# Attention queries on one core: the rotary rows of eight heads gathered into one tile, the split into two parts made from PSUM, and the heads put together again over DRAM

## The chip, the core and the metric

The kernel runs on one core of one Trainium2 chip. The metric is the device time of one launch in microseconds (us). Engines are named as in the profile: PE multiplies matrices, DVE is the vector engine, ACT the scalar engine with its function tables, POOL the GpSimd engine, SP issues DMA transfers. SBUF is the on-chip memory, PSUM the memory into which PE accumulates.

## What is computed

The reference is a decoder trunk of two layers on 1024 tokens of width 1024, in float32. Per layer:

```python
h = rmsnorm(x, norm_mix[l])
q, k, v, u, ug, ga, gb = jnp.split(h @ w_in[l], SPLITS, axis=-1)
q = partial_rope(rmsnorm(q, q_norm[l]), cos, sin)   # 16 heads of 64; the first 16 dims of each rotate
k = partial_rope(rmsnorm(k, k_norm[l]), cos, sin)   # 2 key heads, each for 8 query heads
a_out = sliding_window_attention(q, k, v, sinks[l]) # window 128, blocks of 128 queries
c_out = conformer_conv(u, ug, ...)                  # GLU, causal depthwise conv of width 31, LayerNorm, swish
x = x + (sigmoid(ga) * a_out + sigmoid(gb) * c_out) @ w_out[l]
g, up = jnp.split(rmsnorm(x, norm_ffn[l]) @ w_gate_up[l], 2, axis=-1)
x = x + (silu(g) * up) @ w_down[l]
```

`partial_rope` turns dims 0 to 7 of a head against dims 8 to 15, by an angle that depends on the token, and leaves dims 16 to 63 as they are.

## The kernel before

Everything is kept transposed: features on the 128 partitions, the 1024 tokens along the free axis. To keep float32 accuracy at PE's faster float32r rate, an operand is split into a high and a low part, and a product is made of three matmuls (high x high, high x low, low x high).

A layer has three stages: the input projection with attention and convolution beside it (to about 565 us of the span in layer 0), the merge with the output projection, and the feed-forward part. The change lies in the first.

**The first stage.** The projection makes 34 tiles of 128 output features. Each takes eight steps over the width; a step is six matmuls of 128x512. The list `INPROJ` gives the order of the tiles; K and V come first, two tiles (`TAIL`) are left for after the attention. The program is written along a clock of such steps: `tick()` counts one, `after(n, fn)` and `at(when, fn)` let a piece of the other work be written n steps later. PE's and (in this stage) DVE's instructions are executed in the order in which they are written; those of ACT, POOL and SP are arranged by a scheduler. So what stands where on PE and DVE is fixed by a handful of numbers: `SP` steps between attention units, `S0` steps to the first one, `TS` steps between convolution taps, `QSP`, `QN`, `T1`, `T2`, `TD`, `AD` for the parts of a query tile and of a unit.

**A query tile** (`queries`, L581) holds two whole heads. ACT multiplies by the norm's gain into `q32` and squares the tile into `sqh`. `rope` (L380) copies four strips of 8 rows, swapped, to `rot` by DMA, and POOL multiplies `q32` by the cosine table (L385) and `rot` by the sine table (L386), both 128x1024. Seven steps later DVE adds them (L400). ACT copies each head's 64 rows to the high half of `qs[h]` (L609), and DVE subtracts to get the low half (L613), in the same tile's other 64 partitions, two instructions of 64x1024. Beside that PE sums the squares per head (L391), DVE adds the epsilon (L394), and POOL raises to the power -1/2 (L396), which gives the factor `fq`; from it come its negative `nfq` (L596) and the scaled sinks `sr` (L597, L599).

**An attention unit** (`unit_s`, L622) is two heads by two blocks; 32 units a layer, eight pairs of heads by four. PE writes scores into the one PSUM bank `S` (L633, L634). POOL puts the sinks into a column of `sc` (L636), ACT copies the scores of the own block (L638), DVE those of the block before under a mask (`copy_predicated`, L645), then their greatest (L649) and its negative product (L651); ACT takes the exponential (L653), DVE the reciprocal (L658), ACT scales (L660). PE transposes (`pT`, L669), ACT and DVE split (`ph`, L671; `pl`, L676), POOL masks in four instructions (L681, L684), PE multiplies by the values (`po`, L699), ACT and DVE add the two halves (L704, L705, L711). The next unit's scores go into the same bank `S`, so they wait for L645. The sums of squares use the same bank as `po`.

**The convolution** (`conv_taps`, L485) takes one DVE instruction per tap, 31 for each of four channel tiles (L492, L496): `y = a[:, j:j+T] * w[j] + y`, in SBUF. A channel can begin when its gate tile is projected. LayerNorm over the channels follows: `pmu` (L533) the mean, `pssl` the variance, `pb` (L317) spreads a factor over the partitions.

**Gates** are evicted by DVE times the norm's factor (L721). `fetch` (L120) loads weights (`raw`), ACT casts the high part `wh` (L133), POOL subtracts the low part `wl` (L134). All DMA transfers are issued by SP, in one order.

Of the kernel before, what the change touches and what calls it, by code (L numbers as in the profile page):

```python
# [12 lines left out]
F32 = mybir.dt.float32  # L13
# [8 lines left out]
P = 128  # L22
# [18 lines left out]
V_GK = 17  # L41
V_CB = 18
V_LG = 22
V_LB = 26
V_CWT = 30
V_SK = V_CWT + CC * CW
NV = V_SK + NH
# [5 lines left out]
def trunk(ctx, tc, xT, win, wcv, wout, wgu, wdn, vecs, cosT, sinT, outT):  # L53
# [165 lines left out]
    def when_free(bank, n, fn):  # L219
        def go():  # L220
            if bank in busy:
                after(0.25, go)
            else:
                fn()
        after(n, go)
# [95 lines left out]
    for l in range(DEPTH):  # L321
# [32 lines left out]
        ct = mp.tile([P, T], F32, name="ct")  # L354
        st_ = mp.tile([P, T], F32, name="st_")
        nc.sync.dma_start(ct, cosT)
        nc.sync.dma_start(st_, sinT)
# [6 lines left out]
        sB = [dp.tile([P, T], F32, name=f"sB{l}_{i}") for i in range(8)]  # L364
        att = ExitStack()
        ap_ = pool("ap", 1, None, att)
        rot = ap_.tile([P, T], F32, name="rot")
        nc.gpsimd.memset(rot, 0.0)
# [11 lines left out]
        def rope(src):  # L380
            for h in range(2):
                o = h * HD
                nc.sync.dma_start(rot[o:o + 8], src[o + 8:o + 16])
                nc.sync.dma_start(rot[o + 8:o + 16], src[o:o + 8])
            nc.gpsimd.tensor_tensor(out=src, in0=src, in1=ct, op=ALU.mult)  # L385
            nc.gpsimd.tensor_tensor(out=rot, in0=rot, in1=st_, op=ALU.mult)  # L386

        def headnorm(sq, f):
            pss = ps_o("pssh")
            for b in range(NB):  # L390
                nc.tensor.matmul(pss[:, 2 * b:2 * b + 2], sq[:, b * P:(b + 1) * P], blk1,  # L391
                                 start=True, stop=True)
            ssb = sm.tile([P, NB, 2], F32, tag="ssb", name="ssb")
            nc.vector.tensor_tensor(out=ssb, in0=pss[:, 0:16].rearrange("p (b h) -> p b h", h=2),  # L394
                                    in1=e64.unsqueeze(2).broadcast_to([P, NB, 2]), op=ALU.add)
            nc.gpsimd.tensor_tensor(out=f, in0=ssb.rearrange("p b h -> p (b h)"), in1=mhalf, op=ALU.pow)  # L396
            return ssb

        def rope_add(src):
# [7 lines left out]
        def keys(ps):  # L407
# [4 lines left out]
            after(1 if l else NA + 0.5, lambda: rope(k32))  # L412
            f8 = sm.tile([P, 16], F32, tag="f8", name="f8")

            def norm():
                fk = sm.tile([P, 16], F32, tag="fk", name="fk")
                headnorm(sq, fk)
# [26 lines left out]
            after(9, lambda: rope_add(k32))  # L444
# [40 lines left out]
        def conv_taps():  # L485
            for c in range(CC):
# [4 lines left out]
                y = ap_.tile([P, T], F32, tag="y", bufs=1, name="y")  # L491
# [648 lines left out]
AB = 2  # L1140
# [79 lines left out]
```

## Time and profile before

| | |
|---|---|
| runs | 2714.76 us median of 3 (2712.35 to 2716.32) |
| the profiled execution's own time | 2710.93 us |
| its span, first to last instruction | 2709.2 us |
| PE busy | 2585.2 us, 95% |
| DVE busy | 1876.9 us, 69% |
| POOL busy | 1654.0 us, 61% |
| ACT busy | 1196.4 us, 44% |
| mean granted clock of PE | 0.979 |
| DMA | 379.06 MB, 140 GB/s on the mean |

How to read it: the shares are means over stages that differ. PE is busy for nearly the whole of the span outside the two first stages, and there DVE is idle for a third of the time or more. In the first stages, from about 110 to 490 us and from about 1450 to 1830 us, DVE is busy for over nine tenths. Busy time of PE is not work done: a matmul at a lower clock, or one that is overlapped with its neighbour, counts as busy too. So the number of matmuls per microsecond is the better measure.

### The profile page before, as it was taken

Reading aid. Unit: us, or ns where it says so; the run is one execution under the profiler, and the core shown is the slowest. Engines: PE = TensorE matmul, PEld = TensorE weight load, DVE = VectorE, ACT = ScalarE, POOL = GpSimd, SP = SyncE. Lnnn points to the kernel's source line nnn. Section 1 sums busy time; section 2 is a strip of 40 time slices with the busy share of each in tenths; the row PEclk is TensorE's granted clock in tenths of the full one; section 3 lists DMA queues with packets and bytes.
Section 4 is the critical chain, followed back from the end, with each engine's and each line's share of the span. In section 5 each row is a group of like instructions: output and inputs, shape, how many; then the busy total and the mean of one; then the engine's idle time right before and its main releaser. Section 6 shows DMA issues by size and latency. Waiting matters only on the chain. (4 is left out here: it accounts for less than half of the span.)

```text
span 2709.2 us, 33260 instructions
## 1 busy us (share of the span) xinstructions
PE 2585.2 (95%) x11736; PEld 2112.5 (78%) x11736; DVE 1876.9 (69%) x2053; ACT 1196.4 (44%) x2251; POOL 1654.0 (61%) x1092
## 2 busy tenths in 40 slices
PE   7898898999999999999999989899999999999999
PEld 5777777888787888878877767778887788888887
DVE  6689999652468777855637999995616668778344
ACT  2266566843432323344523665668325222223443
POOL 7368787535356777764535778785252677767544
PEclk8999999999999999999999999999999999999999
DMA  3111111375244454476711111114752444455666
GB/s 129 42 51 34 57 64 51 140 264 215 86 165 149 170 179 156 160 276 218 239 57 43 41 57 49 59 63 156 251 202 97 175 167 145 163 179 191 223 224 210
DMA packets 132359, 379.06 MB, mean 140 GB/s; under 512 B 15136, under 2 KB 15392, under 8 KB 132192
## 3 DMA queue, kind: packets, MB, share of 16 engines
q1 hardware_dynamic: 132048, 376.85, 40.6%
q8 instruction: 92, 1.51, 0.2%
q14 instruction: 75, 0.61, 0.1%
q10 hardware_dynamic: 144, 0.09, 0.0%
HBM read 259.17 MB, written 115.34 MB: 138 GB/s over the span
## 5 line engine op out<-in xcount | busy, mean ns | idle before, releaser
L151 POOL TENSOR_TENSOR plo<-fraw,phi 128x512 fp32r<-128x512 f32 x290 | 423.0, 1467 | 229.2 <-ACT phi L149 214.7
L151 POOL TENSOR_TENSOR plo<-fs,phi 128x512 fp32r<-128x512 f32 x160 | 264.3, 1663 | 253.5 <-ACT phi L149 241.7
L496 DVE SCALAR_TENSOR_TENSOR y<-a,vec,y 128x1024 f32<-128x1024 f32 x240 | 405.7, 1690 | 4.0
L134 POOL TENSOR_TENSOR wl<-raw,wh 128x1024 fp32r<-128x1024 f32 (+1 forms) x100 | 252.4, 2525 | 241.7 <-PE ps L242 196.6
L149 ACT CAST phi<-fraw 128x512 fp32r<-128x512 f32 x444 | 257.6, 618 | 246.4 <-POOL plo L151 131.8
L242 PE MATMUL ps<-hx,wh 128*128 128x512 f32 x1056 | 349.1, 412 | 7.3 <-ACT hx L283 7.3
L242 PE MATMUL ps<-hx,wl 128*128 128x512 f32 x1056 | 335.8, 399 | 4.4 <-POOL wl L134 4.4
L242 PE MATMUL ps<-lx,wh 128*128 128x512 f32 x1056 | 338.0, 401 | 0.8 <-DVE lx L284 0.8
L149 ACT CAST phi<-fs 128x512 fp32r<-128x512 f32 x160 | 95.4, 620 | 534.3 <-DVE fs L164 529.1
L151 DVE TENSOR_TENSOR plo<-fraw,phi 128x512 fp32r<-128x512 f32 x154 | 133.6, 873 | 187.8 <-ACT phi L149 185.5
L847 PE MATMUL b<-plo,phi 128*128 128x512 f32 x616 | 240.8, 391 | 3.9 <-DVE plo L151 3.6
L242 PEld LDWEIGHTS ps<-hx,wl 128*128 128x128 f32 x1056 | 204.8, 194 | 50.0 <-POOL wl L134 4.8
L242 PEld LDWEIGHTS ps<-lx,wh 128*128 128x128 f32 x1056 | 206.1, 195 | 47.9 <-DVE lx L284 1.6
L847 PE MATMUL b<-phi,plo 128*128 128x512 f32 x616 | 239.8, 389 | 0.0
L847 PE MATMUL b<-phi 128*128 128x512 f32 x616 | 239.7, 389 | 0.0
L242 PEld LDWEIGHTS ps<-hx,wh 128*128 128x128 f32 x1056 | 195.6, 197 | 42.9 <-ACT hx L283 7.3
L653 ACT ACTIVATE sc<-sc,nm,fq 128x129 f32<-128x129 f32 x256 | 123.7, 486 | 118.0 <-DVE nm L651 117.6
L133 ACT CAST wh<-raw 128x1024 fp32r<-128x1024 f32 (+1 forms) x100 | 98.2, 982 | 166.0 <-PE ps L242 128.3
L915 POOL TENSOR_TENSOR g<-g,u 128x512 f32<-128x512 f32 (+1 forms) x84 | 129.4, 1558 | 31.9 <-DVE u L968 25.5
L911 DVE TENSOR_TENSOR g<-g 128x512 f32<-128x512 f32 x88 | 102.0, 1159 | 65.7 <-POOL g L915 42.5
L847 PEld LDWEIGHTS b<-plo,phi 128*128 128x128 f32 x616 | 115.6, 188 | 31.6 <-DVE plo L151 7.6
L847 PEld LDWEIGHTS b<-phi 128*128 128x128 f32 x616 | 115.6, 188 | 24.2
(254 smaller groups left out, 6219.2 us busy)
## 6 DMA issues: line engine op xcount, KB each, us to landing
fraw<-wgu SPq DMA_DIRECT2D x88, 512.0 KB
raw<-win SPq DMA_DIRECT2D x68, 512.0 KB
act<-g SPq DMA_DIRECT2D x44, 512.0 KB
dw<-wdn SPq DMA_DIRECT2D x44, 512.0 KB
td<-g SPq DMA_DIRECT2D x44, 512.0 KB
sd<-dw SPq DMA_DIRECT2D x44, 512.0 KB
fraw<-sd SPq DMA_DIRECT2D x88, 256.0 KB
fraw<-td SPq DMA_DIRECT2D x88, 256.0 KB
```

The source lines that it names most:

```text
L133: nc.scalar.copy(wh, raw)
L134: nc.gpsimd.tensor_tensor(out=wl, in0=raw, in1=wh.bitcast(F32), op=ALU.subtract)
L149: nc.scalar.copy(hi, src)
L151: (eng or nc.gpsimd).tensor_tensor(out=lo, in0=src, in1=hi.bitcast(F32), op=ALU.subtract)
L242: nc.tensor.matmul(ps[:, sl], a[:, wc], b[:, sl], start=first and j == 0, stop=last and j == 2)
L496: nc.vector.scalar_tensor_tensor(out=y, in0=a[:, j:j + T], scalar=V(w0 + j), in1=y, op0=ALU.mult, op1=ALU.add)
L653: nc.scalar.activation(sc[:, n], sc[:, n], AF.Exp, bias=nm[:, n:n + 1], scale=fq[:, 4 * j + n:4 * j + n + 1], accum_out=den[:, n:n + 1])
L847: nc.tensor.matmul(ps, w[:, ai * P:(ai + 1) * P], x, start=first and j == 0, stop=last and j == 2, skip_group_check=True)
L911: nc.vector.tensor_tensor(out=o, in0=x, in1=y, op=ALU.subtract)
L915: nc.gpsimd.tensor_tensor(out=g[:, sl], in0=g[:, sl], in1=u[:, sl], op=ALU.mult)
```

## The change

The 1024 query columns of the input projection are put in another order on the host. For each group of eight heads the first of four tiles (m = 0) holds the 16 rotated rows of all eight heads, first dims 0 to 7 of each head, then dims 8 to 15; the other three tiles (m = 1 to 3) hold the eight heads' 48 other rows. So two of eight tiles are rotated instead of eight, with two DMA copies of 64 rows each for the swap.

A tile with m > 0 is split straight from PSUM: ACT writes the high part with the gain (`qh`), DVE the low part in one `scalar_tensor_tensor` from PSUM (`ql`, L623 of the new kernel). A tile with m = 0 goes through SBUF: rotary addition on DVE, high part on ACT, low part on DVE (L640). Both parts are stored to DRAM (L615), and `factors` loads each head's 64 high and 64 low rows into `qs[h]` (L677, L678; eight loads per pair of heads), at the earliest when the pair before it has begun. The layout of `qs` is now the same for both heads of a pair.

The sums of squares come from a product with an indicator of the head (eight columns, `V_IN`) and are added up over the tiles in `ssq`. The cosine and sine tables are now loaded into the buffers of `A`; `rot` is one of the four `t4` buffers. The sinks' column is copied by ACT instead of POOL. The bank `po` is marked as busy from the sum of squares to its addition, and `unit_t` also waits for `ph`. A second buffer `y` is given to the convolution (`YB`). `INPROJ` and the distances are new: first unit 14 steps behind its tiles instead of 16 behind the first, `TD` 9 for 7.5, `T2` 4.5 for 3.5, `TS` 1.3 for 1.42.

The diff, cut to its core:

```diff
@@ rope, headnorm
-        def rope(src):
-            for h in range(2):
-                o = h * HD
-                nc.sync.dma_start(rot[o:o + 8], src[o + 8:o + 16])
-                nc.sync.dma_start(rot[o + 8:o + 16], src[o:o + 8])
-            nc.gpsimd.tensor_tensor(out=src, in0=src, in1=ct, op=ALU.mult)
-            nc.gpsimd.tensor_tensor(out=rot, in0=rot, in1=st_, op=ALU.mult)
+        def rope(src, swaps, ts):
+            rot = t4("rot")
+            if len(swaps) > 2:
+                nc.gpsimd.memset(rot, 0.0)
+            for o, i, n in swaps:
+                nc.sync.dma_start(rot[o:o + n], src[i:i + n])
+            nc.gpsimd.tensor_tensor(out=src, in0=src, in1=ts[0], op=ALU.mult)
+            nc.gpsimd.tensor_tensor(out=rot, in0=rot, in1=ts[1], op=ALU.mult)
+            return rot
...
@@ queries
-            def split():
-                rope_add(q32)
-                for h in range(2):
...
-                    nc.scalar.copy(qs[h][hi], q32[hi])
...
-                    after(1.5 + h, lambda hi=hi, lo=lo, h=h: nc.vector.tensor_tensor(
-                        out=qs[h][lo], in0=q32[hi], in1=qs[h][hi].bitcast(F32), op=ALU.subtract))
...
+        def queries(t, ps):
+            g, m = t // 4, t % 4
+            gain = V(V_GQ + m)
...
+            def store(*x):
+                for w in range(2):
+                    dst = qn[g][w, (m - 1) * P:m * P] if m else qr[g][w].rearrange("s h r t -> (s h r) t")
+                    nc.sync.dma_start(dst, x[w])
+                arrived(g, m)
+            if m:
...
+                nc.scalar.activation(hi, ps, AF.Copy, scale=gain)
+                nc.scalar.activation(sq, ps, AF.Square)
+
+                def rest():
+                    nc.vector.scalar_tensor_tensor(out=lo, in0=ps, scalar=gain, in1=hi.bitcast(F32),
+                                                   op0=ALU.mult, op1=ALU.subtract)
+                    store(hi.bitcast(F32), lo.bitcast(F32))
+                after(QL, rest)
+            else:
...
+                rot = rope(q32, [(0, HD, HD), (HD, 0, HD)], qtab)
+
+                def split():
+                    rope_add(q32, rot)
+                    hi = t4("q0h")
+                    nc.scalar.copy(hi.bitcast(F32R), q32)
+                    after(1.5, lambda: low(hi))
+
+                def low(hi):
+                    nc.vector.tensor_tensor(out=q32.bitcast(F32R), in0=q32, in1=hi, op=ALU.subtract)
+                    store(hi, q32)
+                after(QSP, split)
...
+        def factors(g, p):
+
+            i = 4 * g + p
+            if units_done[0] < 4 * (i - 1):
+                after(1, lambda: factors(g, p))
+                return
...
+            for h in range(2):
+                hh = 2 * p + h
+                for w in range(2):
+                    q = qs[h].bitcast(F32)
+                    nc.sync.dma_start(q[w * HD:w * HD + 16], qr[g][w, :, hh])
+                    nc.sync.dma_start(q[w * HD + 16:(w + 1) * HD], qn[g][w, hh * 48:(hh + 1) * 48])
...
@@ unit_s
-            nc.gpsimd.tensor_copy(sc[:, :, P], sr[:, 2 * j:2 * j + 2].rearrange("p b h -> p (b h)"))
+            nc.scalar.copy(sc[:, :, P], sr[:, 2 * j:2 * j + 2].rearrange("p b h -> p (b h)"))
...
@@ constants
-INPROJ = [W_K, W_V, _u[0], _ug[0], 0, _u[1], _ug[1], 1, _gb[0], _u[2], 2, _ug[2], _ga[0], 3, _gb[1], _ga[1],
-          4, _u[3], _ga[2], 5, _ug[3], _ga[3], 6, _gb[2], _ga[4], 7, _gb[3], _ga[5], _gb[4], _gb[5],
-          _ga[6], _ga[7], _gb[6], _gb[7]]
+INPROJ = [W_K, W_V, _u[0], _ug[0], 1, 0, 4, 2, _u[1], 3, _ug[1], _ga[0], _u[2], 5, _ug[2], _ga[1], 6, _gb[0], _ga[2],
+          7, _ga[3], _u[3], _ug[3], _ga[4], _gb[1], _gb[2], _ga[5], _gb[3], _gb[4], _ga[6], _gb[5], _ga[7],
+          _gb[6], _gb[7]]
...
-TD, AD = 7.5, 5.5
-S0 = 16
+TD, AD = 9, 5.5
+S0 = 14
+YB = 2
+QL, QN2 = 1.5, 1.5
...
-T1, T2, SCB = 2.2, 3.5, 2
+T1, T2, SCB = 2.2, 4.5, 2
...
-TS = 1.42
+TS = 1.3
```

Line numbers in the prediction are those of the kernel before, but for L487, L505, L615, L623, L640, L677, L678 and those in the rows of the new order, which are lines of the changed kernel.

More of the change, by code (lines that the diff above doesn't have):

```diff
@@ L220, in go @@
         def go():
-            if bank in busy:
+            if busy & set(bank.split()):
                 after(0.25, go)
@@ L411, in keys @@
             nc.scalar.activation(sq, ps, AF.Square)
-            after(1 if l else NA + 0.5, lambda: rope(k32))
+            ts = tables(cosT, sinT)
+            swaps = [(h * HD + a, h * HD + b, 8) for h in range(2) for a, b in ((0, 8), (8, 0))]
+            rot = []
+            after(1 if l else NA + 0.5, lambda: rot.append(rope(k32, swaps, ts)))
             f8 = sm.tile([P, 16], F32, tag="f8", name="f8")
@@ L443, in keys @@
             when_free('po', 6, norm)
-            after(9, lambda: rope_add(k32))
+            after(9, lambda: rope_add(k32, rot.pop()))
             when_free('pT', 11, lambda: turn(0))
@@ L620, in trunk, with units @@
+            after(4, finish)
+            at(clock[0] + 5, lambda: qready.update({i: (fq, nfq, sr, qs)}))
+        def units(when):
+            n = units_done[0]
+            if n // 4 not in qready:
+                at(when + 1, lambda: units(when + 1))
+                return
+            unit_s(n // 4, n % 4)
+            units_done[0] += 1
+            if n < 31:
+                at(when + SP, lambda: units(when + SP))
         Av = {}
@@ L772, in trunk @@
             project(j)
-            if idx == 1:
+            if j == W_UG:
                 tap(clock[0] + 2)
-            if idx == 2:
-                start = clock[0] + S0
-                for n in range(32):
-                    at(start + SP * n, lambda n=n: unit_s(n // 4, n % 4))
+            if {W_Q, W_Q + 1} <= set(INPROJ[2:idx + 3]) and j in (W_Q, W_Q + 1):
+                when = clock[0] + S0
+                at(when, lambda: units(when))
             tick()
@@ L1170, in _tables, with _query_rows @@
         st[o + 8:o + 16] = s
-    return ct, st
+    cq, sq = np.tile(c, (16, 1)), np.tile(s, (16, 1))
+    sq[:HD] *= -1
+    return ct, st, cq, sq
+def _query_rows():
+    r = np.arange(NH * HD).reshape(2, 8, HD)
+    out = []
+    for g in range(2):
+        out.append(r[g][:, :16].reshape(8, 2, 8).transpose(1, 0, 2).ravel())
+        out.append(r[g][:, 16:].ravel())
+    return np.concatenate(out)
 def _tiles(w, k, n):
```

132 lines of the change are left out of this document (79 added, 53 removed).

## The prediction, made before the changed kernel was run

> **What bounds the kernel now.** I read the span by stages first. Columns: stretch and length in us, then busy us (and instructions) of PE, its weight loads, DVE, ACT and POOL, the granted clock, the DMA share, GB/s. The stretches are layer 0's attention, twenty of its microseconds in which PE never waits, and layer 1's attention.
>
> ```profile
> 115.00:490.00 375.00, 335.53 (x1659) 277.46 (x1658) 352.07 (x379) 227.44 (x518) 281.31 (x189) 0.95 0.17 55
> 440.00:460.00 20.00, 20.00 (x107) 17.12 (x107) 19.45 (x22) 15.42 (x32) 17.51 (x13) 1.00 0.16 54
> 1456.00:1831.00 375.00, 336.19 (x1658) 277.48 (x1657) 351.80 (x378) 226.80 (x516) 281.73 (x189) 0.95 0.17 55
> ```
>
> Undisturbed, PE does 107 matmuls in 20 us, 5.35 per us. The 1659 matmuls of the long stretch would need 310 us; they take 375. So about **65 us are lost per layer**, and both layers agree. DVE is busy for 352 of the 375 us. Then the waits of PE in that stretch (total, times, longest), and those of DVE:
>
> ```profile
> PE S L633 <- DVE sc L645: 19.2, 8, 5.0
> PE po L699 <- DVE ssb L394: 13.6, 4, 4.6
> ```
>
> ```profile
> DVE y L492 <- DMA yd<-y: 4.0, 1, 4.0
> DVE y L492 <- POOL lsum L502: 2.5, 1, 2.5
> ```
>
> PE waits for DVE: the next unit's S needs the bank that the predicated copy L645 reads, and po needs the bank that L394 reads. DVE itself hardly waits. After a long wait the clock is low too, here in the 4 us behind the longest one, and it is 0.72 in the 4 us after that:
>
> ```profile
> 132.00:136.00 4.00, 3.49 (x12) 3.20 (x13) 2.41 (x5) 2.55 (x6) 0.00 (x0) 0.50 0.02 6
> 136.00:140.00 4.00, 4.00 (x16) 3.18 (x15) 3.15 (x4) 2.86 (x10) 0.43 (x1) 0.72 0.00 0
> ```
>
> What fills DVE, then POOL's wide operations, in the same stretch (count | busy us, mean ns of one | idle before), and the least, median and greatest duration of a tap and of a query split:
>
> ```profile
> L496 DVE SCALAR_TENSOR_TENSOR y<-a,vec,y 128x1024 f32<-128x1024 f32 x113 | 190.3, 1684 | 1.8
> L613 DVE TENSOR_TENSOR qs<-q,qs 64x1024 fp32r<-64x1024 f32 x16 | 37.1, 2318 | 0.4
> L711 DVE TENSOR_TENSOR A<-po,sh 64x256 f32<-64x256 f32 x50 | 20.8, 417 | 0.3
> L649 DVE TENSOR_REDUCE mx<-sc 128x4 f32<-128x516 f32 x28 | 19.3, 691 | 2.8
> L645 DVE COPY_PREDICATED sc<-mprev,S 128x512 f32<-128x512 uint32 (+1 forms) x28 | 18.5, 660 | 0.2
> L676 DVE TENSOR_TENSOR pl<-pT,ph 128x512 fp32r<-128x512 f32 x27 | 18.5, 684 | 0.0
> L651 DVE TENSOR_TENSOR nm<-mx,nfq 128x4 f32<-128x4 f32 x28 | 14.5, 518 | 1.0
> L721 DVE TENSOR_TENSOR g<-ps,R 128x1024 f32<-128x1024 f32 x9 | 11.0, 1225 | 0.7 <-PE ps L242 0.5
> L400 DVE TENSOR_TENSOR q<-q,rot 128x1024 f32<-128x1024 f32 x7 | 8.5, 1215 | 1.7 <-POOL rot L386 1.7
> L596 DVE TENSOR_SCALAR nfq<-fq 128x16 f32<-128x16 f32 x8 | 6.0, 748 | 0.1
> L658 DVE RECIPROCAL ri<-den 128x4 f32<-128x4 f32 x27 | 4.7, 176 | 6.9 <-ACT sc L653 6.4
> ```
>
> ```profile
> L134 POOL TENSOR_TENSOR wl<-raw,wh 128x1024 fp32r<-128x1024 f32 x21 | 63.2, 3008 | 0.8 <-PE ps L242 0.8
> L385 POOL TENSOR_TENSOR q<-q,ct 128x1024 f32<-128x1024 f32 x7 | 23.2, 3314 | 3.6 <-DMA rot<-q 3.6
> L386 POOL TENSOR_TENSOR rot<-rot,st__202 128x1024 f32<-128x1024 f32 x7 | 22.6, 3223 | 0.0
> ```
>
> ```profile
> L496 DVE SCALAR_TENSOR_TENSOR y<-a,vec,y x240: 1254/1534/3455, 91.3 to 1824.3; 128x1024 f32<-128x1024 f32 x120
> ```
>
> ```profile
> L613 DVE TENSOR_TENSOR qs<-q,qs x32: 1220/2726/3429, 113.0 to 1825.7; 64x1024 fp32r<-64x1024 f32 x32
> ```
>
> Operations with a PSUM operand keep their time (L721, 1.225 us); the tap, whose tensors all lie in SBUF, ranges from 1.25 to 3.46. I take it that POOL's wide operations stretch it.
>
> **Calibration.** A unit stands every 6 steps of projection. Two undisturbed S starts give PE's period:
>
> ```profile
> 450.15 0.28 PE L633 MATMUL S<-kh,qs 128*128 128x256 f32 x1
> ...
> 460.70 0.28 PE L633 MATMUL S<-kh,qs 128*128 128x256 f32 x1
> ```
>
> That is 10.55 us. DVE's share per period now: taps 6/1.42 x 1.684 = 7.11; the unit 0.660+0.691+0.518+0.684+2x0.417+0.176 = 3.56; queries (2x2.318+1.215+0.748, and about 0.7 for three smaller ones, an estimate by L596 and L658) = 7.3 per four periods, 1.84; fourteen evictions like L721 over some 26 periods, 0.66. Sum 13.17, so DVE falls back 2.62 us per period, 68 over 26 periods; less 4 us of slack (the copy stands 2.2 of 6 steps behind its S) 64. Measured: 65. The same sum serves for the change.
>
> **The change, part by part** (per layer).
>
> *Splits.* Sixteen L613 go: 37.1 us. Six of eight rotary additions go: 6 x 1.215 = 7.3. Added: six L623, with the PSUM tile as one operand, between 1.225 (L721) and 1.684 (L496): I take 1.25, being nearest to L721, 7.5 in all. Two subtractions of the low half L640, 128x1024, between the 1.22 of L613's least and its mean 2.318: 3.0 for both. The norm's addition has 64 elements instead of 16: nothing I can price above 0.1 us. DVE is relieved by about 32 us.
>
> *POOL.* Twelve of sixteen multiplications L385 and L386 go, 12 x 3.27 = 39 us of POOL. Of the 35 wide ones shown about eleven go, a third; of all that POOL does less, since its masks stay. The taps' mean stands 0.43 above their least; a third less is 0.14. I take 1.534, today's median, 0.15 lower; bounds 1.30 (hardly any contention left) and 1.684 (the remaining POOL work finds the taps instead of L613).
>
> The Trainium skill, "SBUF — State Buffer", section "Who interferes with whom", says that a VectorE instruction with two SBUF inputs and a GpSimd one reading SBUF exclude each other for the whole instruction, while one with a single SBUF input is free. The constant 1.225 of L721 agrees. By that rule up to 39 us of DVE would be freed instead of my 120 x 0.15 = 18, which ends at rival 1.
>
> *The sink copies* go from POOL to ACT, 32 per layer. ACT idles 148 of 375 us, so I cost them at nothing; were that cover gone, ACT's chain sc to pT would grow by their length, and TD = 9 gives it 1.5 steps more.
>
> *Order.* Taps now stand 1.3 steps apart, but the channels' gates come later. DVE, layer 0, at one query tile, before (q is the tile, y the tap):
>
> ```order
> L400 TENSOR_TENSOR q_914<-q_914,rot 128x1024
> L711 TENSOR_TENSOR A<-po,sh 64x256 x2
> L658 RECIPROCAL ri<-den 128x4
> L721 TENSOR_TENSOR g<-ps,R 128x1024
> L496 SCALAR_TENSOR_TENSOR y<-a,vec_95,y 128x1024
> L613 TENSOR_TENSOR qs_927<-q_914,qs_927 64x1024
> L613 TENSOR_TENSOR qs_928<-q_914,qs_928 64x1024
> ```
>
> and DVE now, at a tile without rotated rows:
>
> ```order
> L731 TENSOR_TENSOR nm<-mx,nfq 128x4
> L623 SCALAR_TENSOR_TENSOR ql<-ps,vec_95,qh 128x1024
> L505 SCALAR_TENSOR_TENSOR y<-a,vec_95,y 128x1024
> L756 TENSOR_TENSOR pl<-pT,ph 128x512
> L505 SCALAR_TENSOR_TENSOR y<-a,vec_95,y 128x1024
> ```
>
> Three wide operations have become one. By INPROJ and TS channel 0's taps fill steps 38 to 78, channels 1 and 2 94 to 174, channel 3 190 to 230; in the two pauses of 16 steps DVE catches up. Per period in channels 1 and 2: 4.615 x 1.534 = 7.08, the unit 3.56, seven evictions and three L623 over 13.3 periods 0.93, small ones 0.42: 11.99, against 10.55. That is 1.44 x 13.3 = 19 less 4: 15. Channel 3: 1.43 x 6.67 = 9.5 less 4: 5. Channel 0 has few units: 2. Together 22. The second y buffer also removes DVE's 4.0 + 2.5 us of waiting; I leave that in hand.
>
> *The end of the stage.* PE in layer 0, the last rows before the two projections left over; before (pb spreads LayerNorm's factor, pT and po are a unit):
>
> ```order
> L317 MATMUL pb<-dg,onesmat 128x512
> L242 MATMUL ps<-hx_143,wh 128x512 x2
> L242 MATMUL ps<-lx_144,wh 128x512 x2
> L242 MATMUL ps<-hx_143,wl 128x512 x2
> L669 MATMUL pT<-ident,sc 128x128 x4
> L699 MATMUL po<-mo,vv 128x256 x2
> ```
>
> and now:
>
> ```order
> L749 MATMUL pT<-ident,sc 128x128 x4
> L318 MATMUL pb<-dg,onesmat 128x512 x2
> L780 MATMUL po<-mo,vv 128x256 x2
> L780 MATMUL po<-ph,vv 128x256
> L780 MATMUL po<-pl,vv 128x256
> ```
>
> No projection stands between them any more, so PE waits for the chain from pT to pb and po. Its links, from before's end of the stage:
>
> ```profile
> 542.05 0.57 ACT L671 CAST ph<-pT 128x512 fp32r<-128x512 f32 x1
> ...
> 545.56 0.59 ACT L318 COPY lsum<-pb 128x512 f32<-128x512 f32 x1 [2.17 <-PE pb L317]
> ```
>
> ```profile
> 535.50 0.86 DVE L711 TENSOR_TENSOR A<-po,sh 64x256 f32<-64x256 f32 x2
> ...
> 536.47 1.44 DVE L310 TENSOR_TENSOR dg<-ident,rln 128x1024 f32<-128x1024 f32 x1
> ```
>
> 0.57+0.68 (L676)+0.86+1.44+0.59 = 4.1, with handovers 5. The clock row above lost 0.5x4+0.28x4 = 3.1 us after a 5.0 us wait. I take 8; bounds 5 and 12. The Trainium skill, "TensorE: Matmul & The Clock Gate", section "What's actually happening", speaks against the change here: an idle window of about 3.4 us halves the clock until as long a busy one. By it 1.7 us would follow, the trace shows 3.1; the sum would be 2.8 us lower.
>
> *The detour over DRAM.* Store, then load: SP issues zd's store, and ACT's cast starts on what came back:
>
> ```profile
> 561.59 0.32 SPq L565 DMA_DIRECT2D zd<-y  x1
> ```
>
> ```profile
> 567.51 1.05 ACT L794 CAST zh<-z 128x1024 fp32r<-128x1024 f32 x1 [0.67 <-DMA z<-zd]
> ```
>
> 5.9 us. From the second pair on the loads have 20 steps of lead or more. For the first pair the low half stands at step 56.5 and S at 62: 5.5 steps of 1.1 us (six matmuls at 5.35 per us) to 1.76 (10.55/6), 6 to 10, against 1.5 + 5.9. The other rotated tile's swap stands on SP behind that store, and on DVE the rotary addition that waits for it has unit 0's copy behind it; the keys' swaps now wait for a memset of their buffer. For all three I take 2 us of waiting on PE; bounds 0 and 8. The traffic, 16.8 MB a layer against the 21 MB that now take 0.17 of the DMA engines, I cost at nothing.
>
> **Sum.** Lost per layer: 22 + 8 + 2 = 32 instead of 65, 33 gained, 66 over both. The profiled execution took 2710.9 us, 3.8 under the median of the runs shown: 2645 on its scale, **2649** against the median.
>
> **Rivals.**
>
> *1. PE becomes the bound.* If taps fall to 1.30, DVE's period is 10.9 and only 1 us a layer is left of the 22: 65 - 11 = 54, twice 108, time 2607. For it: sums of DVE's free times. Against: wl alone keeps POOL busy for 63 us of the stretch. The Trainium skill's rule on the shared port, cited above, would lead here.
>
> *2. The relief goes to POOL.* Taps stay at 1.684: period 12.7, channels 1 and 2 lose 24, channel 3 10, channel 0 3, with tail and start 47: 18 gained, 36 in all, 2679; with a worse tail and start (12 and 8) and lateness at po's bank, near 2702 and beyond. For it: denser taps.
>
> *3. Slower: SP's queue.* SP issues in order. Each of eight tiles a layer now has a store that waits for DVE's low half, and weight loads are queued behind it (first pair, layer 0; before, a tile had four short copies there):
>
> ```order
> L126 DMA raw<-win 128x1024
> L615 DMA qr_0_228<-q0h 128x1024
> L615 DMA qr_0_228<-q_727 128x1024
> L389 DMA rot<-q_810 64x1024 x2
> L677 DMA qs_826<-qr_0_228 16x1x1024 x2
> L677 DMA qs_827<-qr_0_228 16x1x1024
> L678 DMA qs_827<-qn_0_230 48x1024
> ```
>
> The next tile's swap and pair 0's loads also stand behind that store. A weight's load and its cast today:
>
> ```profile
> 445.79 0.33 SPq L125 DMA_DIRECT2D raw<-win  x1
> ...
> 456.76 1.06 ACT L133 CAST wh<-raw 128x1024 fp32r<-128x1024 f32 x1
> ```
>
> 11 us apart, of which I estimate 3 (half of 5.9) for the transfer. So a store late by over 8 us decides. At 6 us per tile, slow clock included, 48 a layer: 33 - 48 = -15, twice, 2745. Against: DVE's lag came to 5.0 us at most.
>
> **How the numbers follow.** Forecast 0.50 (2625 to 2672), rival 1 0.18, rival 2 0.22, rival 3 0.10. 0.2%, about 5.4 us, is what a measurement can tell from no change. Rival 2 lends 0.04 to "no change", rival 3 0.01: faster 0.86, same 0.05, slower 0.09. The range 2597 to 2702 leaves out rival 3, the worst of rival 2 and the best of rival 1, under 0.2 together.
>
> **What would show it.** S behind L645 near zero in channel 0 and the pauses, and a few us late within channels 1 to 3; taps' mean 1.5 to 1.6; L623 at 1.25; a gap of 5 us on PE between pT and po before the last two projections, with a clock near 0.5 behind it; 1659 matmuls in about 332 us instead of 375. Wrong if PE waits for wl or wh (rival 3), if DVE falls under 85% (rival 1), or if taps stay at 1.68 (rival 2).

## The result: slower by 0.6%, and the profile after

| | before | after |
|---|---|---|
| median of the runs | 2713.56 us (2709.97 to 2716.32, 4 runs) | 2728.93 us (2727.06 to 2731.61, 4 runs) |
| ratio | | 1.0059, 95% interval 1.0044 to 1.0074 |
| the profiled execution's own time, span | 2710.93, 2709.2 | 2730.0, 2728.3 |
| mean granted clock | 0.979 | 0.970 |

The forecast was 2649, with 2597 to 2702 as its range and 0.09 for slower. The two stretches of 375 us first, after the change (columns as in the prediction), and twenty microseconds each out of a pause of the taps and out of a run of them:

```profile
115.00:490.00 375.00, 344.98 (x1724) 293.43 (x1724) 305.53 (x367) 228.36 (x551) 228.08 (x156) 0.94 0.29 96
1456.00:1831.00 375.00, 344.51 (x1734) 293.11 (x1735) 309.07 (x364) 221.69 (x534) 222.59 (x151) 0.95 0.30 96
```

```profile
380.00:400.00 20.00, 19.77 (x106) 16.89 (x105) 9.20 (x21) 13.59 (x36) 15.45 (x12) 1.00 0.46 144
420.00:440.00 20.00, 17.29 (x82) 14.47 (x82) 19.64 (x26) 13.70 (x34) 11.57 (x10) 0.91 0.44 133
```

DVE is busy for 305.5 us instead of 352.1, POOL for 228 instead of 281: the relief came. But PE did only 65 matmuls more in the same time, so that 1659 of them took some 361 us, where the prediction's sign was 332. DVE's mean hides two states: in the pauses of the taps it is half idle, in the runs it is nearly as full as before (88% busy from 200 to 380 us, where it had been 96%). What PE waits for in layer 0's whole stage:

```profile
PE po L780 <- POOL pl L764: 12.4, 7, 3.5
PE pssh L398 <- DVE A L792: 8.1, 4, 3.7
PE pb L318 <- DVE dg L311: 6.6, 1, 6.6
PE ps L243 <- ACT zh L874: 3.8, 2, 3.1
PE S L713 <- DMA qs<-qn: 3.4, 1, 3.4
PE S L713 <- DVE sc L725: 2.5, 1, 2.5
PE S L713 <- DMA qs<-qr: 2.3, 1, 2.3
PE pssl L300 <- DVE A L792: 1.9, 1, 1.9
PE po L780 <- POOL mo L761: 1.3, 1, 1.3
```

The 19.2 us of S behind the predicated copy are 2.5 now, the 13.6 of po behind the sums of squares are gone. In their place po waits for POOL's last mask, pssh for the bank that DVE's A (L792) has to empty, S for its first queries, and at the end pb waits for the spread and the merge for its input zh. DVE's groups that answer to the sum of the prediction, in the first stretch:

```profile
L505 DVE SCALAR_TENSOR_TENSOR y<-a,vec,y 128x1024 f32<-128x1024 f32 x109 | 182.1, 1671 | 1.6
L623 DVE SCALAR_TENSOR_TENSOR ql<-ps,vec,qh 128x1024 fp32r<-128x1024 f32 x5 | 6.4, 1283 | 5.6 <-ACT sqh L620 5.5
L640 DVE TENSOR_TENSOR q<-q,q0h 128x1024 fp32r<-128x1024 f32 x2 | 2.5, 1225 | 0.6 <-ACT q0h L636 0.6
```

The new operations cost what was forecast or less. The taps did not: 1.671 us on the mean, against 1.684 before.

**Where the time went.** Three landmarks divide a stage: the first S, the S of the last pair's last unit, and the first merged eviction of DVE. Before, in layer 0, on PE and DVE:

```profile
117.87 0.23 PE L633 MATMUL S<-kh,qs 128*128 128x128 f32 x1
524.13 0.28 PE L633 MATMUL S<-kh,qs 128*128 128x256 f32 x1
580.78 1.22 DVE L808 TENSOR_TENSOR gb<-ps,gb 128x1024 f32<-128x1024 f32 x1 [4.42 <-PE ps L242]
```

and after:

```profile
133.84 0.30 PE L713 MATMUL S<-kh,qs 128*128 128x128 f32 x1 [2.32 <-DMA qs<-qr]
518.89 0.28 PE L713 MATMUL S<-kh,qs 128*128 128x256 f32 x1
587.73 1.23 DVE L888 TENSOR_TENSOR gb<-ps,gb 128x1024 f32<-128x1024 f32 x1 [3.80 <-PE ps L243]
```

In steps of projection the first S stands at 55 before and at 62 after, the last one at 241 and 248. Seven steps are 9.5 us (an undisturbed one begins at 117.33 and the next at 118.69 in the trace after the change, 1.36 us). So of the 16.0 us by which S comes later, 9.5 are work moved ahead; the same 9.5 are missing behind the last S. Three sums of squares now stand ahead of the first S instead of one, and five behind it instead of seven:

```profile
114.18 1.85 PE L398 MATMUL pssh<-vec,sqh 128*128 128x8 f32 x16
```

So another 3.7 us of work moved from the units to the start. Then, per layer:

- **start**: beside the seven steps 6.0 and 6.4 us more between the keys' transpose pk and S. Of these 3.7 are the moved sums of squares, and 2.3 and 2.6 are S waiting for its first loads. In layer 1 another 6.1 were lost ahead of pk, 3 of them where the keys' transposes wait 4.2 us instead of 1.2;
- **units**: 406.3 us became 385.0, in layer 1 384.0: 21 to 22 less, 3.7 of it the moved sums of squares, so 18 gained. S's second wait for loads (3.4 and 3.1 us) lies in here;
- **end**: 56.6 became 68.8 with 9.5 us less to do, in layer 1 56.3 became 67.9: 21 to 22 lost.

The sums are 6 and 11 us lost, 18 of the span's 19.1.

The end, on PE:

```profile
538.67 0.60 PE L749 MATMUL pT<-ident,sc 128*128 128x128 f32 x4
545.82 2.05 PE L318 MATMUL pb<-dg,onesmat 128*128 128x512 f32 x2 [6.55 <-DVE dg L311]
577.10 0.73 PE L243 MATMUL ps<-zh,wh 128*128 128x512 f32 x2 [3.08 <-ACT zh L874]
```

```profile
540.00:550.00 10.00, 3.51 (x5) 1.34 (x5) 3.07 (x4) 3.02 (x4) 3.36 (x4) 0.59 0.10 28
580.00:600.00 20.00, 19.51 (x72) 15.24 (x73) 12.14 (x10) 6.20 (x8) 3.52 (x3) 0.85 0.80 277
```

The bare gap between pT and pb is there as forecast, 6.55 us, with the clock at 0.59 around it. What the forecast did not have is the second hole: LayerNorm's spread also stands eight steps later, its output is late for the merge, zh is waited for and the clock falls again. The waits are 13.5 us of the 21; the rest goes with a mean granted clock of 0.85 over these 68.8 us.

### The profile page after: what moved, and what is told of

Same layout as the page of the kernel before. It is cut to its first block, busy times and chain, and to the rows that moved or that the text cites. A ratio compares the mean times of both kernels' runs of the same rounds, so it can differ in the third digit from the quotient of the medians.

```text
span 2728.3 us, 33345 instructions
## 1 busy us (share of the span) xinstructions
PE 2587.4 (95%) x11736; PEld 2127.2 (78%) x11736; DVE 1777.9 (65%) x2025; ACT 1186.0 (43%) x2295; POOL 1514.1 (55%) x1004
## 5 line engine op out<-in xcount | busy, mean ns | idle before, releaser
L135 POOL TENSOR_TENSOR wl<-raw,wh 128x1024 fp32r<-128x1024 f32 (+1 forms) x100 | 240.5, 2406 | 314.6 <-PE ps L243 194.1
L505 DVE SCALAR_TENSOR_TENSOR y<-a,vec,y 128x1024 f32<-128x1024 f32 x240 | 395.7, 1649 | 3.8
L761 POOL TENSOR_SCALAR_AFFINE_SELECT mo<-ph 128x512 fp32r<-128x512 f32 x64 | 54.7, 855 | 156.7 <-ACT ph L751 156.7
```

The source lines that it names most:

```text
L135: nc.gpsimd.tensor_tensor(out=wl, in0=raw, in1=wh.bitcast(F32), op=ALU.subtract)
L505: nc.vector.scalar_tensor_tensor(out=y, in0=a[:, j:j + T], scalar=V(w0 + j), in1=y, op0=ALU.mult, op1=ALU.add)
L761: nc.gpsimd.affine_select(out=mo, in_=src.bitcast(F32), pattern=[[0, 4], [1, P]], compare_op=ALU.is_ge, fill=0.0, base=0, channel_multipli ...
```

## The experiments

Two theories. **End**: the units' gain is real, and the start and above all the stage's end take it back. **Contention**: the units themselves gain less than half of the forecast 43 us, since the taps inherit the collisions of DVE with POOL. They don't exclude each other; the rivals are that the detour over DRAM, the sink copies or the bank of po are the cause. One table, layer 0, in us (start from pk to the first S, units and end as above; with before's landmarks seven steps on, a level start is 49.9, or 53.6 with the moved sums of squares, and a level end 47.1). Each ratio is to runs of the kernel before taken beside that version. e10 and e11 start one step earlier, e14 two later. In e1, e5, e6, e13, e14 and e16 another 2.3 us of LayerNorm's matmuls (pssl and the first half of pb) stand ahead of the last S, in the units instead of the end; in e11 it is pssl alone.

| kernel | start | units | end | median, ratio to before |
|---|---|---|---|---|
| before | 40.4 | 406.3 | 56.6 | |
| after | 55.9 | 385.0 | 68.8 | 1.0059 (1.0044 to 1.0074) |
| e1 gates early | 56.3 | 403.7 | 54.7 | 2738.52, 1.0093 (1.0073 to 1.0113) |
| e2 before, late end | 49.9 | 421.9 | 67.4 | 2789.64, 1.0285 (1.0265 to 1.0305) |
| e3 after, low weights zero | 60.4 | 360.8 | 66.6 | 2667.62, one run |
| e4 start | 56.1 | 388.4 | 65.8 | 2729.12, 1.0060 (1.0044 to 1.0076) |
| e5 even taps | 62.0 | 393.6 | 56.9 | 2731.15, 1.0066 (1.0051 to 1.0081) |
| e6 even, tail 1 | 62.2 | 393.4 | 48.8 | 2716.55, 1.0013 (1.0001 to 1.0025) |
| e7 tail 1 | 57.2 | 384.8 | 67.5 | 2735.13, 1.0092 (1.0068 to 1.0116) |
| e8 sinks on POOL | 56.0 | 385.8 | 65.6 | 2730.22, 1.0069 (1.0050 to 1.0088) |
| e9 before, low weights zero | 40.4 | 380.5 | 56.4 | 2643.09, one run |
| e10 tiles 0, 1 | 58.3 | 386.9 | 65.9 | 2734.13, one run |
| e11 e6 with tiles 0, 1 | 59.2 | 393.2 | 53.9 | 2717.03, 1.0013 (1.0001 to 1.0024) |
| e12 before, splits later | 40.4 | 413.0 | 56.4 | 2724.72, 1.0047 (1.0030 to 1.0064) |
| e13 pssh in pT's bank | 63.3 | 394.9 | 48.3 | 2711.58, 1.0004 (0.9995 to 1.0013) |
| e14 more lead | 62.0 | 411.7 | 47.1 | 2746.52, 1.0130 (1.0110 to 1.0149) |
| e15 loads of 8 rows | 54.0 | 387.9 | 65.8 | 2728.24, 1.0060 (1.0046 to 1.0074) |
| e16 best | 60.1 | 388.8 | 49.2 | 2702.85, 0.9966 (0.9954 to 0.9977) |

### The stage's end: e1, e2, e7

e1, the last channel's projections earlier:

```diff
-          7, _ga[3], _u[3], _ug[3], _ga[4],
+          _u[3], _ug[3], 7, _ga[3], _ga[4],
```

> The changed kernel with the last channel's two projections (u3, ug3) moved ahead of the query tile and the gate that stood before them, so that LayerNorm's sums and its spread stand at steps 241, 247 and 249 instead of 255 and 256, with projections between them; the units stand where they did. If the stage's end is what gives the gain back (from the last pair's S to the first merged eviction 68 us for 24 steps, against 56.5 us for 31 steps before, some 21 us a layer), most of that goes: the 6.6 us wait of pb for dg and the 3 us wait for zh vanish, and the last unit's wait for its masks of about 4 us stays: 10 to 15 us a layer, 2700 to 2710 in all. If the end costs only the 8 us a layer that the prediction gave it, and the loss lies in the detour over DRAM or in the units, it gains under 5 us a layer: 2720 or more.

The end did what the theory said, 68.8 to 54.7, and the waits for dg and zh are gone; of the end's waits only 6.4 us of po for the last A and 1.7 for its masks are left. But the units took 19 us more (2 of them LayerNorm's matmuls), and the median rose by 10. e1 has filled up the pause of the taps; the same twenty microseconds as above, in e1:

```profile
380.00:400.00 20.00, 17.33 (x88) 14.63 (x87) 14.41 (x17) 8.88 (x25) 14.21 (x9) 0.91 0.39 130
420.00:440.00 20.00, 15.45 (x74) 12.54 (x73) 19.60 (x23) 13.22 (x30) 14.12 (x9) 0.92 0.34 110
```

88 and 74 matmuls instead of 106 and 82. The pauses that made the end late were what let DVE catch up. So 2700 to 2710 failed by a thing that the theory of the end did not have.

e2, the late end put into the kernel before:

```diff
-INPROJ = [... 4, _u[3], _ga[2], 5, _ug[3], _ga[3], 6, _gb[2], _ga[4], 7, ...
+INPROJ = [... 4, _ga[2], 5, _u[3], _ga[3], 6, _ug[3], _gb[2], _ga[4], 7, ...
-S0 = 16
+S0 = 23
```

> The kernel before with nothing of the change but its end: the units start 7 steps later (S0 23 instead of 16) and the last channel's projections come later, so that the last S stands at step 248, LayerNorm's sums at 256 and its spread, the last pT and po all at step 256 with no projection between. If the late end costs what the accounts of the two traces say, some 21 us a layer, this is slower by 35 to 45 us: 2750 to 2758, with waits of pb for dg of 6 us and of ps for zh of 3 us. If the end costs 8 us a layer, 2730. If it costs nothing by itself, since the projections only change places, 2714.

With the seven steps counted, the end costs 67.4 + 9.5 - 56.6 = 20.3 us (19.5 in layer 1) in a kernel that has nothing else of the change: that is the end's price, shown. It agrees with the 21 to 22 of the changed kernel, though the largest hole lies at another place, pssl behind A:

```profile
573.27 3.54 PE L299 MATMUL pssl<-onesC,s 128*128 128x1 f32 x16 [7.49 <-DVE A L711]
```

The units took 16 and 18 us more as well, which was not expected and put the whole above the expected 2750 to 2758.

e7, one projection more beside the last units, one less behind them:

```diff
-TAIL = 2
+TAIL = 1
```

> The changed kernel itself with one projection kept for after the last unit instead of two: the last unit and LayerNorm's spread (6.6 us wait of pb, 2 us at half clock) get eight steps of projections beside them, at steps 257 to 263, but only one projection, 11 us, is left to cover LayerNorm's output, its way over DRAM and its splits, some 25 us from the spread to zh. If the bare drain is the whole of the end's 21 us, 8 to 12 us a layer are gained: 2706 to 2714. If what counts is that LayerNorm's output is late for the merge, the wait only moves to zh, 12 to 15 us there instead of 3, and the time stays within 5 us of 2729 or rises.

The gap at pb went, and came back whole at zh:

```profile
580.74 1.22 PE L243 MATMUL ps<-zh,wh 128*128 128x512 f32 x2 [14.73 <-ACT zh L874]
```

So the bare drain is not the end's bound: LayerNorm's chain to zh is, and the gap at pb lay in its shadow.

### Contention: e3, e9, e12

e3 on the changed kernel, e9 on the kernel before:

```diff
-            nc.gpsimd.tensor_tensor(out=wl, in0=raw, in1=wh.bitcast(F32), op=ALU.subtract)
+            nc.gpsimd.memset(wl.bitcast(F32), 0.0)
```

> The changed kernel, but the low halves of the mixing weights (wl, L135) are filled with zeros by GpSimd instead of being subtracted from raw and wh: GpSimd's widest work in the stage, 59 us of it reading two tensors in SBUF, becomes 22 short fills; all matmuls stay. If the taps keep their mean of 1.67 us because GpSimd's wide operations still shut them out, the mean falls to 1.35 to 1.50, the waits of po for pl and of pssh for A (20 us in layer 0) fall under 8, and the time from the first S to the last pair's S falls from 385 us to 350 to 365. If the taps are long for another reason, or PE's lateness comes from its own order (pssh in the bank of po), the mean stays over 1.6 and that time over 378.

> The kernel before with the low halves of the mixing weights (L134) filled with zeros by GpSimd instead of subtracted, as e3 did to the changed kernel (which fell by 61 us, its units from 385 to 361 us a layer). If GpSimd's wide work lengthens DVE's two-tensor operations in both kernels alike, taps and query splits L613 (2.3 us) both shorten here, the units fall from 406 to 365 to 385 us and the whole to 2640 to 2670, level with e3 or ahead of it: then the change's relief of DVE is worth little once that contention is gone. If the contention only began to matter with the change, the units stay over 395 us and the whole over 2690.

e3, then e9, taps and splits in the first stretch:

```profile
L505 DVE SCALAR_TENSOR_TENSOR y<-a,vec,y 128x1024 f32<-128x1024 f32 x107 | 155.4, 1452 | 1.5
```

```profile
L496 DVE SCALAR_TENSOR_TENSOR y<-a,vec,y 128x1024 f32<-128x1024 f32 x107 | 174.7, 1633 | 1.7
L613 DVE TENSOR_TENSOR qs<-q,qs 64x1024 fp32r<-64x1024 f32 x14 | 17.4, 1243 | 0.4
```

In the changed kernel POOL's weight subtraction lengthens the taps (1.671 to 1.452 without it); in the kernel before it lengthened mostly the splits (2.318 to 1.243), which stood where the next weights are split. By these means, an estimate, the subtraction cost 17 us on the 16 splits and 6 on the 113 taps before, and 24 on the 109 taps after: what the splits had carried, the taps carry now. The units fall by 24 and 26 us. The difference between the two kernels' units is the same with this contention or without it, 21 and 20 us; and without it the kernel before is ahead by 25 us, 2643 against 2668, since the changed kernel's end is as it was (66.6) and its start 4 us longer. Two limits: PE's waits for masks and bank in e3 fell only from 20.5 to 11.5 us, not under 8; and the fills also shorten POOL's own queue (59.1 us of subtraction became 22.9 of fills), so how much of the 24 us came by shorter taps and how much by earlier masks is not separated.

e12, the splits of the kernel before moved away from the weights:

```diff
-QSP = 7
+QSP = 9
```

> The kernel before with its rotary additions and query splits two steps later (QSP 9 instead of 7), so that they no longer stand where GpSimd subtracts the next weights. If DVE's and GpSimd's two-input operations simply exclude each other, the time is only passed on: L613 falls from 2.3 towards 1.3 us, the taps' mean rises from 1.68 to 1.75 or more, and the whole stays at 2705 to 2720. If the collision can be avoided by the placing, L613 falls, the taps stay, the units fall by 12 to 20 us a layer: 2675 to 2695, and most of what the change wanted of the splits is had without it.

```profile
L496 DVE SCALAR_TENSOR_TENSOR y<-a,vec,y 128x1024 f32<-128x1024 f32 x113 | 200.2, 1771 | 1.7
L613 DVE TENSOR_TENSOR qs<-q,qs 64x1024 fp32r<-64x1024 f32 x14 | 17.9, 1281 | 0.4
L400 DVE TENSOR_TENSOR q<-q,rot 128x1024 f32<-128x1024 f32 x7 | 10.2, 1463 | 0.0
```

L613 fell by 1.04 us each, 16.6 over 16; the taps rose by 0.087 each, 9.8 us over 113, and the additions by 0.25. Contention was passed on, not removed, and the units became 7 us slower. The Trainium skill, "SBUF — State Buffer", section "Who interferes with whom", has it that a VectorE instruction with two SBUF inputs and a GpSimd one that reads SBUF exclude each other for the whole instruction, and that a GpSimd write alone does not. The traces agree: in e3 a tap beside a fill alone took 1.28 us (16 taps), the same as beside nothing on POOL (109), and in the changed kernel 2.28 us beside a weight subtraction alone (17).

### The start: e4, e10, e14, e15

e4 changes SP's order and the keys' fill; in the diff `rk` is `rot` allocated and filled ahead of the keys' projections:

```diff
-INPROJ = [W_K, W_V, _u[0], _ug[0], 1, 0, 4, 2,
+INPROJ = [W_K, W_V, _u[0], _ug[0], 1, 0, 2, 4,
+        rk = t4("rot")
+        nc.gpsimd.memset(rk, 0.0)
```

> The changed kernel with its two starts mended: the query tiles come in the order 1, 0, 2, 4, so that the second rotated tile's swap no longer stands on SP ahead of the first pair's loads, and the zero fill of the keys' rotation buffer stands ahead of the keys' projections. If the first pair's detour costs 6.4 us a layer through SP's order, the two DMA waits of S (2.3 and 3.4) fall to 2 us together and S starts 4 to 6 us sooner in each layer; if the fill is what makes the keys' transposes wait 4.2 us in layer 1 instead of 1.2, that is 5 us there. Together 13 to 17 us: 2712 to 2716. If the detour's wait is the transfer's own time and not SP's order, the waits stay over 5 us and only the keys' 5 us come: 2724.

The keys' wait in layer 1 fell to 1.16 us; the first S's waits fell from 5.7 to 3.9 us, but only behind the first S, so the start stayed at 56.1; and the units gave 3 and 7 us back, with po behind POOL's masks at new places (2.7 us at 165). Nothing was left.

e10 has the rotated tile first (`0, 1, 4, 2` for `1, 0, 4, 2`):

> The changed kernel with the first two query tiles in the order 0, 1 instead of 1, 0, so that the rotated tile, whose rotation, split, store and load take longest, comes eight steps sooner; the first S stands at step 61 instead of 62. If S's waits of 2.3 and 3.4 us are the detour of that tile, they vanish and S starts 5 to 8 us sooner in each layer (56 us behind pk in the changed kernel, then 48 to 51), with nothing lost behind it: 2712 to 2722. If something else on SP or in the transfers holds the loads, the waits stay over 4 us together and S starts at most 2 us sooner.

S waits 5.7 us all the same. So the tile's own rotation and split were not what S waited for. That it waits for the pair's loads is read from their landing. In the changed kernel the last load of the first pair lands at 137.54 and S goes on at 137.68; in e10 it is 136.63 and 136.72, where the view of waits names a weight load that had landed before; in e13 and e14, where it names nothing, 139.21 and 139.30, 138.95 and 139.04. In the changed kernel's trace the last loads, the second pair's among them, run alone from 135 to 140 us (packets, MB, share of 16 engines):

```profile
q1 hardware_dynamic: 73, 0.26, 12.9%
```

12.9% of 16 engines are two, and 0.26 MB in 5 us 52 GB/s. The Trainium skill, "DMA: Bandwidth & Descriptors", section "Why a DMA increments its semaphore by 16 and not by 1", says that a transfer uses the largest number of engines up to 16 that divides the slowest dimension of both its sides. Here one side has two strips of 8 rows, so that is two, and the trace agrees. e15:

```diff
-                    nc.sync.dma_start(q[w * HD:w * HD + 16], qr[g][w, :, hh])
+                    for s in range(2):
+                        nc.sync.dma_start(q[w * HD + 8 * s:w * HD + 8 * s + 8], qr[g][w, s, hh])
```

> The changed kernel with each load of a head's 16 rotated rows (64 KB, two strips of 8 rows) issued as two loads of 8 rows. In the changed kernel's trace these loads run alone from 135 to 140 us at 52 GB/s and 12.9% of the DMA engines, two of 16, while S waits for its pair. If two engines are what makes the first pair's loads late, eight rows spread over eight engines: S's waits of 2.3 and 3.4 us fall under 2 us together and S starts 3 to 6 us sooner in each layer; nothing else changes: 2716 to 2724. If SP's issue time or the write before them is what holds them, the four more issues a pair make it later by 2 us: 2728 to 2736.

The start gained 2 us in both layers, the units lost 3 and 4: no difference that can be measured. S still waits 3.7 us: SP now issues the pair's last load at 133.86 instead of 130.74. e14 changed the lead on top of e13 (`S0 = 17`):

> e13 with the units two steps later (S0 17, the first S at step 64 instead of 62). In e6 the first S waited 8.4 and 9.4 us for its pair. If that is lead alone, two steps of projections, 2.7 us, come out of the wait and the start is level (62 us behind pk as in e6), with a shorter wait and a better clock behind it: 0 to 4 us a layer gained, 0 to 8 below e13. If the loads only start later too, since they wait for SP or for tiles that move with the units, the wait stays at 8 us and each layer loses 3 us: 4 to 8 above e13.

The wait fell from 9.7 to 5.6 us, so lead is a part of it, but the units, standing otherwise against the taps, lost 17 us. In the changed kernel, e4, e5, e6, e13, e15 and e16 the start is 53.6 us and the first S's wait (2.3, 2.4, 8.4, 8.6, 9.7, 0.4 and 6.5), to 0.1 us: nothing else is lost there. So the detour's price in the changed kernel is S's two waits, 5.7 and 5.8 us in the two layers, and the clock behind them (0.50 from 136 to 140 us). Lead, two engines and SP's issues all have a part in it; how they divide, and why the loads land later in e5, e6 and e13, stays open. No run kept the second pair's loads back.

### The sinks and the bank of po: e8, e13

e8 is the changed kernel with `nc.gpsimd.tensor_copy` for the sinks again:

> The changed kernel with only the 64 small sink copies back on GpSimd, as before the change. By the prediction they cost nothing on ACT: the time stays within 5 us of 2729. If they hold up S's eviction on ACT (the copy waits for sr, 4.8 us once), it is up to 10 us faster; if on GpSimd they delay the masks that po waits for (12 us a layer), 5 to 15 us slower.

No difference that can be measured: what they cost doesn't depend on the engine.

e13 is e6 (below) with pssh in the other bank:

```diff
-            pss = ps_o("pssh")
+            pss = ps_pT("pssh")
-            when_free('po', QN, norm)
+            when_free('pT', QN, norm)
```

> e6 (taps spread, one projection kept back, the keys' fill ahead) with pssh in the bank of pT instead of that of po, held there until DVE has added it. In e6 pssh waits 4.5, 3.5 and 4.7 us for A in layer 0, each with a slow clock behind it. If the sharing of po's bank is the cause, these go and 12 to 20 us a layer come in the units (393 to 375 or 380): 2680 to 2692, faster than both kernels. If DVE's lag is the cause, another wait takes their place (pT for ssq, or pssh for pl) and the units stay over 388: 2706 to 2718.

First e6's wait, then e13's:

```profile
PE pssh L396 <- DVE A L790: 12.7, 3, 4.7
```

```profile
PE pssh L396 <- DVE pl L754: 8.9, 3, 3.7
```

Another reader of the other bank, on the same late engine, and the 12 to 20 us a layer did not come: the units are 1.5 us longer in layer 0 and 5.5 shorter in layer 1. So it is DVE's lag for the most part; the bank only names it.

### Put together: e5, e6, e11, e16

e5 spreads the convolution's projections evenly and takes the taps at before's pace (with e4's keys' fill):

```diff
-TS = 1.3
+TS = 1.42
-INPROJ = [... 1, 0, 4, 2, _u[1], 3, _ug[1], _ga[0], _u[2], 5, _ug[2], _ga[1], 6, _gb[0], _ga[2], 7, _ga[3], _u[3], _ug[3], ...
+INPROJ = [... 1, 0, 4, 2, _u[1], _ug[1], 3, _ga[0], _u[2], 5, _ug[2], _ga[1], 6, _u[3], _ga[2], 7, _ug[3], _ga[3], _gb[0], ...
```

> The changed kernel with the conv projections spread so that the taps run without a pause at before's pace (one per 1.42 steps, LayerNorm's sums at step 242, its spread at 248 and 250), the same units, and the zero fill of the keys' buffer ahead as in e4. e1 gained 14 us a layer at the end and lost 19 in the units, with the taps of two channels bunched at 1.3 steps. If bunching is what lost them, the units come near the changed kernel's 385 us or under (375 to 388) and the end stays at 55: 13 us a layer and 5 for the keys, 2695 to 2710 in all. If any pace without the pauses lets DVE fall behind, since the taps stay at 1.65 us beside GpSimd's work, the units take 398 to 406 us and the whole stays at 2725 to 2738.

e6 is e5 with `TAIL = 1`:

> e5 with one projection kept for after the last unit instead of two, so that the last two units have projections between their steps. If the 6 to 7 us wait of po for the last A and the slow clock behind it are what is left of the end, it is 7 to 10 us a layer shorter than e5; since LayerNorm's spread is done by step 250, its output should be back from DRAM in time. If the merge then waits for LayerNorm's output instead, it is level with e5 or up to 10 us a layer longer.

e11 is e6 with `0, 1, 4, 2` for `1, 0, 4, 2`:

> e6 (taps spread evenly, one projection kept back, the keys' fill ahead) with the query tiles in the order 0, 1 as well. e6 ended its stage in 49 us, as good as before's 56.5 less seven steps, but its first S waited 8.4 and 9.4 us for the first pair. If that wait is the rotated tile's detour and goes, 7 to 9 us a layer come: 2698 to 2704, faster than both kernels. If it only turns into a wait of a unit behind it, for the taps on DVE, the whole stays at 2712 to 2718.

The taps of e5, in the same stretch as above:

```profile
L503 DVE SCALAR_TENSOR_TENSOR y<-a,vec,y 128x1024 f32<-128x1024 f32 x109 | 173.1, 1588 | 1.3
```

Even taps are shorter, 1.588 us, and still cost the units 9 us against the changed kernel instead of e1's 19; they give the end 12. With LayerNorm early, the projection that e7 moved in vain is worth 6 to 8 us a layer (e6): the end is down to 48.8, where 44.8 would be level. In e11 S comes 3 us sooner, and the end is 5 us longer. e16 is e13 with e15's loads:

> e13 (taps spread, one projection kept back, the keys' fill ahead, pssh in the bank of pT) with the same loads of 8 rows. e13's first S waits 9.7 and 8.9 us for its pair. If two engines are the cause, that falls under 4 us and 6 to 10 us a layer come with the better clock behind it: 2690 to 2700, faster than both kernels. If another wait for DVE takes its place, 2704 to 2712.

2702.85 us, 0.9966 of before (0.9954 to 0.9977): the only version faster than both, though short of the expected 2700. Its first S still waits 6.5 us for the loads. SP issues them one by one while S waits until 136.86, and since a pair has eight, the second pair's are among these twelve; that the issuing holds S up is argued, not tried:

```profile
132.00 5.69 SPq L676 DMA_DIRECT2D qs<-qr  x12
```

## Why the prediction was wrong

**The step that failed first: "I take 1.534" for the taps.** The working let a third of POOL's wide work vanish and a third of the taps' excess with it. That part came about: without the weight subtraction a tap takes 1.633 us in the kernel before (e9) and 1.452 in the changed one (e3), 0.18 less, where the prediction took 0.15. But the taps inherited the collisions with the weight subtraction that the splits had carried: its part in a tap rose from 0.05 to 0.22 us. So the taps stayed at 1.671: what they gained by the multiplications that are gone they lost to the collisions that the 16 splits had carried (17.6 us of excess, 2.318 less 1.22 each). e3, e9 and e12 show it. That was the condition of rival 2, to which the prediction gave 0.22, with 37 us left in the units instead of 22.

**Its second half: masks and bank unpriced.** By a floor of 31 of the prediction's periods of 10.55, and 1.85 more for each pssh on the way (seven before, five after), the units lose 66 us before and 49 after, and 37 would have been the lag alone. Of the other 12 us, 3.4 are S's second wait for its loads. The 12.4 us of po behind POOL's last mask had been 2.3. One of them, DVE, POOL and PE:

```profile
370.29 6.42 DVE L505 SCALAR_TENSOR_TENSOR y<-a,vec,y 128x1024 f32<-128x1024 f32 x3
```

```profile
370.72 3.35 POOL L813 TENSOR_TENSOR g<-g,A 128x1024 f32<-128x1024 f32 x1
374.01 1.62 POOL L764 TENSOR_SCALAR_AFFINE_SELECT pl<-pl 128x512 fp32r<-128x512 f32 x1
```

```profile
375.69 0.39 PE L780 MATMUL po<-pl,vv 128*128 128x256 f32 x1 [2.08 <-POOL pl L764]
```

A gate's product stands ahead of the last mask, and three taps and two POOL operations take turns. That this would come once S no longer waited is argued from such rows; no run took the gate's product away.

**What stays open in the units.** The taps' price is not the whole of it. In e5 the taps are at 1.588, a good part of the forecast fall, DVE is busy for 79% of the units' time, and they still took 393.6 us. So a sum of DVE's load alone does not give what PE loses, since PE also waits for chains that go through POOL and ACT. And in e2, the kernel before with its units begun at step 62 and its last channel late, as in the changed kernel, they took 421.9, 37 us more than there. How much of the shortfall lies in where the units stand against the taps, and not in the taps' price, no run separates.

**The end: 8 us, and it was 21.** The gap's size was right (5 forecast, 6.55 measured, slow clock behind it). The term left out what hangs behind the gap: LayerNorm's spread stands at 256 instead of 248, its way over DRAM to zh is as long as ever, and seven steps of cover had gone to the start. e2 prices this at 20 in a kernel without the rest, and e7 shows that closing the gap alone gives nothing.

**The detour: 2 us, and it was 5.7** in S's two waits, within its bounds of 0 to 8, with a slow clock behind them that the term left out. The keys' transposes in layer 1 wait 3 us longer for the fill, which the prediction had named and put under the same 2; e4 took back 2.9 of the 6.1 lost there, and the rest is not explained (the same stretch is 3.6 us longer in e12 too, which changes nothing in it).

**What was right.** The calibration (65 lost before), DVE's relief by the splits (in the stretch 37.1 and 6.0 us gone, 6.4 and 2.5 added: 34 against 32, and the prediction's own terms add up to 33.9; the new operations at 1.283 and 1.225 against 1.25 and 1.5 taken), POOL's, S behind L645 (2.5 us), the sinks' copies (e8), and no sign of rival 3: PE waits for no weight in layer 0's stage.

**In sum**, per layer: forecast 43 in the units, less 2 and 8, 33 gained; measured 18 in the units, where S's second wait is already in, less 2 to 9 at the start and 21 to 22 at the end: 6 to 11 lost. The sign "DVE under 85%" that was to show PE as the bound was a bad one: DVE is at 81% and still late, since it is nearly full in the runs and half idle in the pauses.

## What to carry to other kernels

Relieving an engine is worth what its full stretches lose, not what its mean shows; and where two engines exclude each other, taking away the operation that carried the collisions hands them to the next one. A stage that is started later by some steps needs those steps at its end: count the filler left behind the last unit, and the whole chain that hangs on it, before crediting the middle. Then look at the shape of every small load that a first consumer waits for, and at how long its issues take.

## What the runs showed of the hardware that was not expected

- A wide two-input operation of POOL and one of DVE, both from SBUF, lengthen each other where they meet: 64x1024 splits took 1.24 us where the weights were only filled (e9) and 2.32 among weight subtractions, and in the kernel before a subtraction took 2.45 us on the mean beside no tap or split and 3.04 beside one. Moved away (e12), the splits left 60% of what they gained to the taps (9.8 of 16.6 us over 16).
- A load of 64 KB in two strips of rows moved at 52 GB/s on two DMA engines, while the row of 580 to 600 us above has 277.
- Short waits cost nearly as much again in clock: PE waited 28 us between the first and the last S, none longer than 3.7, and at a mean granted clock of 0.94 some 23 of the 385 us went as well, an estimate. A wait of 1.94 us at 532.92 was enough for a clock of 0.50 from 535 to 538 us.
